# Gate and up products of a feed-forward layer by Strassen's scheme, on one core

## The chip, the cores and the metric

The kernel runs on one core of a Trainium2 chip. The core has a matrix engine (PE, with its loads of weights as PEld), a vector engine (DVE), a scalar engine (ACT), GpSimd (POOL) and a queue of transfers that SyncE (SP) issues. The metric is the device time of one execution in microseconds, less is better.

## What is computed

A trunk of two layers on 512 tokens of width 1024. Each layer has a feed-forward layer (FFN), a mixer and a second FFN, each on the RMS-normalised x and added to x.

```python
def rmsnorm(x, g):
    y = xf * lax.rsqrt(jnp.mean(xf * xf, axis=-1, keepdims=True) + EPS)
    return (y * g.astype(jnp.float32)).astype(x.dtype)
def swiglu_ffn(x, w_gu, w_down):
    gate, up = jnp.split(x @ w_gu, 2, axis=-1)
    return (jax.nn.silu(gate) * up) @ w_down
```

D_FF is 2816. The first mixer (stage ab) is a recurrence beside a chunked mLSTM, the second (stage nsa) is attention with a compressed, a selected and a window branch.

## The kernel before

The stages run in the order f0a, ab, f0b, f1a, nsa, f1b; four of them are FFNs. x lies transposed in eight tiles X of 128 channels x 512 tokens. Every product keeps fp32 accuracy by splitting both operands into a high part (a copy rounded to the matmul's type, on ACT) and a low part (the difference, on DVE), and by three matmuls, high x high, high x low and low x high: `mm3`, L169 to L171 of the profile.

An FFN goes through 22 tiles j of 128 hidden channels. For each j two weight tiles of 128 x 1024 (gate and up) are brought in by `wload`: one transfer of 512 KB, the high part on ACT (L164), the low part on DVE (L165). Then 16 `mm3`, that is 48 matmuls of 128 x 512, make the gate and the up rows. x stands in these products without its norm; 1/rms of each token (the row R, 128 x 512, the same on each partition) is multiplied to the results in `hidden` (L235, L237), where Silu, the product and the split into high and low follow. The sum for R (`rms_sum`, L133) and its spread along the free axis (`rms_row`, L145) stand on PE between the products of j=1, so that the next stage's products need not wait for the norm. The down product then takes all 22 hidden tiles, for each of the eight tiles of X 66 matmuls, and the result is added to X (L274). For the next stage `prep` (L99, L100) splits the new X and `square` (L109, L111) adds its squares, on ACT and POOL.

A scheduler with priorities puts the instructions of each engine in order; where the code says `manual_schedule(engines=PE_ONLY)`, PE's order is the written one. `high_priority(offset=...)` in the loads makes weights come ahead. Within an engine, order is fixed when the program is built, and each instruction waits for what it needs.

In nsa the scores of 128 queries are computed by `scores`: for each of two heads a selected and compressed part (`slc`) and a window part (`win`), each as a product of 128 rows (high parts, L755, L762) and one of 64 rows (low parts, L756, L763) into one PSUM tile, 64 of each kind. Between them stand turns of other products.

## Time and profile before

| | |
|---|---|
| median of 3 runs | 2132.83 us (2132.11 to 2137.12) |
| profiled execution, from first to last instruction | 2130.4 us |
| PE busy | 2097.7 us, 98% |
| PEld, DVE, ACT, POOL busy | 78%, 48%, 38%, 13% |
| mean granted clock of PE | 0.990 |
| DMA, mean over the span | 85 GB/s |

A busy share is the time in which an engine had an instruction under way. The chain is followed back from the last instruction, each step to what released it. The groups by line sum instructions of the same kind, with their mean length and the idle time ahead of them. Times in the timeline and in the windows count from the first instruction.

### The profile page before, as it was taken

How to read it: one execution, taken by the hardware profiler on the slowest of the kernel's cores; microseconds unless marked ns; L12 is line 12 of the kernel's file. 1: busy time of each engine (PE TensorE's matmuls, PEld its weight loads, DVE VectorE, ACT ScalarE, POOL GpSimd, SP SyncE). 2: the span in 40 equal slices, each digit the busy share in tenths (PEclk: the TensorE clock that was granted, in tenths of full speed). 3: DMA queues.
4: the chain of work that ended last, by engine and by line, in shares of the span. 5: the costliest groups of instructions: out<-in, count | busy, mean ns of one | idle time of the engine just before them, and what ended most of it. 6: DMA issues, size and time to landing. Idle time of an engine off the chain costs nothing.

```text
span 2130.4 us, 23902 instructions
## 1 busy us (share of the span) xinstructions
PE 2097.7 (98%) x9304; PEld 1672.3 (78%) x9304; DVE 1016.8 (48%) x1685; ACT 803.0 (38%) x1368; POOL 271.8 (13%) x290
## 2 busy tenths in 40 slices
PE   8999999989999999999999999999999999999997
PEld 7888888767888888888888888877766678888886
DVE  5444423587644444333444432324767664444332
ACT  4322322454532323223322322235777753323221
POOL 3000000242020000000000000003555430000001
PEclk9999999999999999999999999999999999999998
DMA  4232233222132232332232233331000023222331
GB/s 149 90 99 95 91 91 100 89 77 82 54 99 94 95 99 90 91 100 97 89 99 97 89 100 91 129 109 37 23 11 21 16 75 102 95 99 89 96 95 67
DMA packets 53970, 181.66 MB, mean 85 GB/s; under 512 B 6113, under 2 KB 6881, under 8 KB 53857
## 3 DMA queue, kind: packets, MB, share of 16 engines
q1 hardware_dynamic: 53712, 180.05, 26.6%
q8 instruction: 73, 1.20, 0.2%
q14 instruction: 41, 0.33, 0.0%
...
## 4 chain that ended last, share of the span: by engine, by line
PE 95%; DVE 2%; issue 1%; ACT 1%; POOL 1%; DMA 0%; SPq 0%; POOLq 0%; ACTq 0%; DVEq 0%
PE ps L169 20%; PE ps L171 19%; PE ps L170 19%; PE pt L171 8%; PE pt L169 8%; PE pt L170 8%; PE px L801 2%; PE pt L817 2%; PE pt L594 2%; PE ps L756 1%; PE ps L763 1%; PE pt L818 1%; PE ps L220 1%; PE ps L221 1%; PE ps L222 1%
## 5 line engine op out<-in xcount | busy, mean ns | idle before, releaser
L164 ACT ACTIVATE whi<-raw 128x1024 fp32r<-128x1024 f32 (+2 forms) x340 | 345.8, 1019 | 1062.8 <-PE ps L170 654.0
L165 DVE TENSOR_TENSOR wlo<-raw,whi 128x1024 fp32r<-128x1024 f32 (+2 forms) x310 | 368.3, 1189 | 349.9 <-ACT whi L164 344.7
L169 PE MATMUL ps<-x,whi 128*128 128x512 f32 x1008 | 407.0, 404 | 1.9 <-ACT x L99 1.9
L171 PE MATMUL ps<-x,wlo 128*128 128x512 f32 x1008 | 399.3, 396 | 0.0
L170 PE MATMUL ps<-x,whi 128*128 128x512 f32 x1008 | 395.9, 393 | 0.4 <-DVE x L100 0.3
L171 PE MATMUL pt<-x,wlo 128*128 128x512 f32 x704 | 278.3, 395 | 2.0 <-POOL wlo L951 2.0
L170 PE MATMUL ps<-h,whi 128*128 128x512 f32 x704 | 277.4, 394 | 0.0
L169 PE MATMUL ps<-h,whi 128*128 128x512 f32 x704 | 277.2, 394 | 0.0
L169 PE MATMUL pt<-x,whi 128*128 128x512 f32 x704 | 276.8, 393 | 0.0
L171 PE MATMUL ps<-h,wlo 128*128 128x512 f32 x704 | 276.4, 393 | 0.0
L170 PE MATMUL pt<-x,whi 128*128 128x512 f32 x704 | 275.6, 392 | 0.0
L111 POOL TENSOR_TENSOR acc<-acc,t 128x512 f32<-128x512 f32 x48 | 71.4, 1487 | 1461.4 <-ACT t L109 1447.0
L169 PEld LDWEIGHTS ps<-x,whi 128*128 128x128 f32 x1008 | 189.8, 188 | 46.5 <-issue 2.8
L170 PEld LDWEIGHTS ps<-x,whi 128*128 128x128 f32 x1008 | 190.1, 189 | 44.1 <-DVE x L100 1.9
L171 PEld LDWEIGHTS ps<-x,wlo 128*128 128x128 f32 x1008 | 189.8, 188 | 44.2 <-issue 0.2
L237 DVE TENSOR_TENSOR t<-pt,R 128x512 f32<-128x512 f32 x88 | 60.8, 691 | 279.5 <-PE pt L171 279.4
L171 PEld LDWEIGHTS pt<-x,wlo 128*128 128x128 f32 x704 | 132.3, 188 | 32.8 <-POOL wlo L951 2.5
L170 PEld LDWEIGHTS pt<-x,whi 128*128 128x128 f32 x704 | 132.4, 188 | 31.5
L171 PEld LDWEIGHTS ps<-h,wlo 128*128 128x128 f32 x704 | 132.3, 188 | 31.0
L169 PEld LDWEIGHTS ps<-h,whi 128*128 128x128 f32 x704 | 132.1, 188 | 31.3
L170 PEld LDWEIGHTS ps<-h,whi 128*128 128x128 f32 x704 | 132.1, 188 | 30.4
L169 PEld LDWEIGHTS pt<-x,whi 128*128 128x128 f32 x704 | 132.3, 188 | 29.6
...
## 6 DMA issues: line engine op xcount, KB each, us to landing
...
raw<-nsa_out SPq DMA_DIRECT2D x16, 256.0 KB, 2.7
X<-xT SPq DMA_DIRECT2D x8, 256.0 KB, 5.3
```

The lines of the kernel that those rows point to most:

```text
L111: nc.gpsimd.tensor_add(acc, acc, sq)
L164: nc.scalar.activation(hi[:, :n], raw[:, :n], AF.Copy)
L165: (eng or nc.vector).tensor_sub(lo[:, :n], raw[:, :n], hi[:, :n].bitcast(F32))
L169: nc.tensor.matmul(ps, wh, xh, start=start, stop=False)
L170: nc.tensor.matmul(ps, wh, xl, start=False, stop=False)
L171: nc.tensor.matmul(ps, wl, xh, start=False, stop=stop)
L220: nc.tensor.matmul(pss[t], xh, wh, start=k == 0, stop=False)
L221: nc.tensor.matmul(pss[t], xl, wh, start=False, stop=False)
L237: nc.vector.tensor_mul(t2, pu, R)
L594: nc.tensor.matmul(p2[m][:, :155].rearrange("p (g n) -> p g n", g=5), w[:, q * 256 + m * P:q * 256 + (m + 1) * P], tt[:, :, n:n + 8 * 30 + ...
L801: nc.tensor.transpose(px[:kk, (2 * m + r) * P:(2 * m + r + 1) * P], pt[r][b][:, off:off + kk], ident)
L817: nc.tensor.matmul(po[0][:, :2 * P], v, ph[:kk, ms], start=n == 0 and m == 0, stop=False)
```

## The change

The gate and up products of the pairs j = 2 to 21 become Strassen's scheme (Winograd's form): gate and up weights of a j are one matrix of 2 x 2 quarters (k halves x gate or up), x is one of 2 x 2 quarters (k halves x token halves), and 7 products of quarters take the place of 8. j = 0 and 1 stay as before. After them x is normalised with R on DVE, and seven operands are made of its quarters, B11, Q7, Q6, B21, Q4, Q5, B22 (`quarters`), each in a high and a low part. On the side of the weights `sload` brings in 1 MB for each j in three transfers into a pair of r buffers (ra, rc; two such pairs in turn), makes four combinations on POOL (L289 to L292), and splits all in four steps, three of 128 x 1024 and one of 128 x 512, on ACT (L303) and DVE (L304), into five slots used in turn. A product is 12 matmuls of 128 x 256. Partial results are read from PSUM by ACT (L387, L389, L393) and added by DVE (L395, L384, L380); the last product of a pair, B22, is put between Q7 and Q6 of the next pair. The down product goes in three parts, after j = 7, 15 and 21, each added to X. The norm's sum goes two products earlier (13 for 15) except in f0a. In nsa, `both` issues the two high products first and the two low ones after, in two PSUM tiles. Comments that the change strips are left out here.

```diff
-        def ffn(wgu, wd, x, hb, nxt, first=None):
+        QS = ("B11", "Q7", "Q6", "B21", "Q4", "Q5", "B22")
+        WS = {"B11": (0, 0), "Q7": (0, 1), "Q6": (1, 0), "B21": (1, 1), "Q4": (2, 0), "Q5": (2, 1), "B22": (3, 0)}
+        H = T // 2
+        def quarters(qb, tmp):
+            Q = {}
+            xn = [blk(b, F32, f"xn{b}")[:, :4 * T].rearrange("p (k t) -> p k t", k=4) for b in tmp[:2]]
+            sm = blk(tmp[2], F32, "qs")[:, :4 * T].rearrange("p (s k t) -> p s k t", s=2, k=4)
+            B = {f"B{h + 1}{t + 1}": xn[h][:, :, t * H:(t + 1) * H] for h in range(2) for t in range(2)}
+            gname = plan[current[0]]
+            def norm(h):
+                for k in range(4):
+                    nc.vector.scalar_tensor_tensor(xn[h][:, k], X[4 * h + k], col(gname, 4 * h + k), R,
+                                                   op0=OP.mult, op1=OP.mult)
+            def split(name, src, neg):
+                t = blk(qb[QS.index(name)], F32R, f"q{name}")
+                hi, lo = (t[:, n * 4 * H:(n + 1) * 4 * H].rearrange("p (k t) -> p k t", k=4) for n in range(2))
+                nc.scalar.activation(hi, src, AF.Copy, scale=-1.0 if neg else 1.0)
+                if neg:
+                    nc.vector.scalar_tensor_tensor(lo, src, -1.0, hi.bitcast(F32), op0=OP.mult, op1=OP.subtract)
+                else:
+                    nc.vector.tensor_sub(lo, src, hi.bitcast(F32))
+                Q[name] = hi, lo
+            def sums(n):
+                if n == 0:
+                    nc.vector.tensor_sub(sm[:, 0], B["B12"], B["B22"])
+                    split("Q7", sm[:, 0], False)
+                if n == 1:
+                    nc.gpsimd.tensor_sub(sm[:, 1], B["B12"], B["B11"])
+                    nc.vector.tensor_sub(sm[:, 0], B["B22"], sm[:, 1])
+                    split("Q6", sm[:, 0], False)
+                if n == 2:
+                    split("Q5", sm[:, 1], False)
+                    nc.gpsimd.tensor_sub(sm[:, 1], B["B21"], sm[:, 0])
+                    split("Q4", sm[:, 1], False)
+            return Q, [lambda: norm(0), lambda: split("B11", B["B11"], True), lambda: norm(1), lambda: sums(0),
+                       lambda: sums(1), lambda: split("B21", B["B21"], True), lambda: sums(2),
+                       lambda: split("B22", B["B22"], True)]
+        def sload(w, rb, wx):
+            with tc.high_priority(offset=SAHEAD):
+                n = turns[0]
...
+                nc.sync.dma_start(ra[:, 0:4:3], w[0].rearrange("p (s c) -> p s c", s=2))
+                nc.sync.dma_start(rc[:, 3], w[1][:, :T])
+                nc.sync.dma_start(rc[:, 0], w[1][:, T:])
+                nc.gpsimd.tensor_add(ra[:, 1], ra[:, 0], rc[:, 3])
+                nc.gpsimd.tensor_add(rc[:, 1], rc[:, 0], rc[:, 3])
+                nc.gpsimd.tensor_add(ra[:, 2], ra[:, 0], rc[:, 1])
+                nc.gpsimd.tensor_add(rc[:, 2], ra[:, 3], ra[:, 2])
+                out = []
+                for src, m in ((ra[:, 0:2], 2), (ra[:, 2:4], 2), (rc[:, 0:2], 2), (rc[:, 2:3], 1)):
+                    at = turns[0] % 5
...
+                    nc.scalar.activation(hi[:, :m * T], src, AF.Copy)
+                    nc.vector.tensor_sub(lo[:, :m * T], src, hi[:, :m * T].bitcast(F32))
...
-            at = 19 if first else 15
+            at = 19 if first else 13
...
-            for j in range(JT):
+            for j in range(2):
...
+            Q, steps = quarters(qb, hb[1:4])
+            for n, f in enumerate(steps):
+                f()
+                if n in (4, 6):
+                    hidden(*wait.pop(0))
+            def product(ps, W, name, start):
+                wh, wl = W[name]
+                xh, xl = Q[name]
+                for k in range(4):
+                    ks = slice(k * P, (k + 1) * P)
+                    mm3(ps[:, :H], wh[:, ks], wl[:, ks], xh[:, k], xl[:, k], start and k == 0, k == 3, not start)
+            def pair(j, left, more):
+                W = sload(wgu[j], rb, wx)
+                a, b, e = psum(), psum(), psum2()
...
+                def last():
+                    product(a, W, "B22", False)
+                    nc.scalar.activation(t1[:, hi], a[:, :H], AF.Silu, scale=-1.0)
+                    nc.vector.tensor_mul(t2, t1, t2)
+                    down(j, t2)
+                def turn():
+                    product(a, W, "Q5", False)
+                    nc.vector.tensor_add(t2[:, hi], a[:, :H], t2[:, hi])
+                def other():
+                    product(e, W, "Q4", False)
+                    nc.vector.tensor_add(t2[:, lo], e[:, :H], t2[:, lo])
+                product(a, W, "B11", True)
+                nc.scalar.activation(t1[:, lo], a[:, :H], AF.Copy)
+                product(e, W, "Q7", True)
+                nc.scalar.activation(t2[:, hi], e[:, :H], AF.Copy)
+                if left:
+                    left()
+                product(a, W, "Q6", False)
+                nc.scalar.activation(t2[:, lo], a[:, :H], AF.Copy)
+                product(b, W, "B21", True)
+                nc.vector.tensor_add(t1[:, lo], b[:, :H], t1[:, lo])
+                nc.scalar.activation(t1[:, lo], t1[:, lo], AF.Silu, scale=-1.0)
+                if more:
+                    other()
+                    turn()
+                    return last
+                turn()
+                other()
+                last()
+            for j0 in range(0, JT, NH):
+                j1 = min(JT, j0 + NH)
+                with tc.manual_schedule(engines=PE_ONLY):
+                    left = None
+                    for j in range(max(2, j0), j1):
+                        left = pair(j, left, j < j1 - 1)
...
+                for i in range(KT):
+                    ps = psum()
+                    hi, lo = wload(wd[i, :, j0 * P:j1 * P], (j1 - j0) * P)
...
+                    nc.vector.scalar_tensor_tensor(X[i], ps, 0.5, X[i], op0=OP.mult, op1=OP.add)
+                    if j1 == JT:
+                        nxt(i)
...
-                def slc(r):
...
-                def win(r):
...
+                def both(r):
                     q = QH[g][2 * r + par]
...
+                    p1, p2 = psum(), psum()
+                    nc.tensor.matmul(p1[:, :n1], q[:, qs], KH[g][:, :n1], start=True, stop=False)
+                    nc.tensor.matmul(p2[:, :n2], q[:, qs], KWH[g][:, w0:w0 + n2], start=True, stop=False)
+                    nc.tensor.matmul(p1[:, :n1], q[rr, qs], KL[g // 2][rr, :n1], start=False, stop=True)
+                    nc.tensor.matmul(p2[:, :n2], q[rr, qs], KWL[g // 2][rr, w0:w0 + n2], start=False, stop=True)
...
-                return [lambda: slc(0), lambda: win(0), lambda: slc(1), last]
...
+                return [lambda: both(0), last]
```

In f0a the transfers for pair 2 stand first on SP, ahead of X and the first weights. In the code after the change, lines have moved: `mm3` is L171 to L173, the low part of `wload` is L166, `hidden` is L327 to L330 with `down` at L321 and L322.

DVE in f0b, from behind the row sum on. Before, in order (t1 and t2 are the hidden rows, R the row of 1/rms, wlo the low part of weights, h the low part of hidden rows):

```order
L235 TENSOR_TENSOR t1_4261<-ps_4123,R_84 128x512
L237 TENSOR_TENSOR t2_4262<-pt_4124,R_84 128x512
L235 TENSOR_TENSOR t1_4269<-ps_4202,R_84 128x512
L238 TENSOR_TENSOR t2_4262<-t1_4261,t2_4262 128x512
L165 TENSOR_TENSOR wlo_4286<-raw_4283,whi_4285 128x1024
L241 TENSOR_TENSOR h4_4100<-t2_4262,h4_4100 128x512
L237 TENSOR_TENSOR t2_4270<-pt_4203,R_84 128x512
L238 TENSOR_TENSOR t2_4270<-t1_4269,t2_4270 128x512
L165 TENSOR_TENSOR wlo_4350<-raw_4347,whi_4349 128x1024
L241 TENSOR_TENSOR h4_4100<-t2_4270,h4_4100 128x512
```

After, at the same place, from the fourth of the eight normalisations on (xn8, xn9 are the halves of normalised x, X its tiles, r0 and r1 the r buffers, q... the operands by their names, qs the differences); the three normalisations ahead of it are like it:

```order
L248 SCALAR_TENSOR_TENSOR xn8_5392<-X3_73,prm_78,R_84 128x512
L248 SCALAR_TENSOR_TENSOR xn9_5393<-X4_74,prm_78,R_84 128x512
L248 SCALAR_TENSOR_TENSOR xn9_5393<-X5_75,prm_78,R_84 128x512
L304 TENSOR_TENSOR wlo_5460<-r0_5446,whi_5459 128x1024
L256 SCALAR_TENSOR_TENSOR qB11_5399<-xn8_5392,qB11_5399 128x1024
L248 SCALAR_TENSOR_TENSOR xn9_5393<-X6_76,prm_78,R_84 128x512
L248 SCALAR_TENSOR_TENSOR xn9_5393<-X7_77,prm_78,R_84 128x512
L327 TENSOR_TENSOR t1_5415<-ps_5254,R_84 128x512
L263 TENSOR_TENSOR qs_5394<-xn8_5392,xn9_5393 128x1024
L329 TENSOR_TENSOR t2_5416<-pt_5255,R_84 128x512
L304 TENSOR_TENSOR wlo_5464<-r1_5447,whi_5463 128x1024
L258 TENSOR_TENSOR qQ7_5407<-qs_5394,qQ7_5407 128x1024
```

and directly behind these:

```order
L256 SCALAR_TENSOR_TENSOR qB21_5423<-xn9_5393,qB21_5423 128x1024
L267 TENSOR_TENSOR qs_5394<-xn9_5393,qs_5394 128x1024
L330 TENSOR_TENSOR t2_5416<-t1_5415,t2_5416 128x512
L304 TENSOR_TENSOR wlo_5567<-r0_5554,whi_5566 128x1024
L258 TENSOR_TENSOR qQ6_5412<-qs_5394,qQ6_5412 128x1024
L322 TENSOR_TENSOR h7_5238<-t2_5416,h7_5238 128x512
L258 TENSOR_TENSOR qQ5_5426<-qs_5394,qQ5_5426 128x1024
L327 TENSOR_TENSOR t1_5433<-ps_5333,R_84 128x512
L329 TENSOR_TENSOR t2_5434<-pt_5334,R_84 128x512
L256 SCALAR_TENSOR_TENSOR qB22_5441<-xn9_5393,qB22_5441 128x1024
L330 TENSOR_TENSOR t2_5434<-t1_5433,t2_5434 128x512
L258 TENSOR_TENSOR qQ4_5430<-qs_5394,qQ4_5430 128x1024
```

The hidden rows of j = 0 and 1 now stand among the normalisations and the operands' low parts, and three weight splits stand there too.

POOL in f0b behind the last of the next norm's sums. Before, nothing follows there until the next stage's norm. After:

```order
L266 TENSOR_TENSOR qs_5394<-xn8_5392 128x1024
L289 TENSOR_TENSOR r0_5678<-r0_5678,r1_5679 128x512
L290 TENSOR_TENSOR r1_5679<-r1_5679 128x512
L291 TENSOR_TENSOR r0_5678<-r0_5678,r1_5679 128x512
L292 TENSOR_TENSOR r1_5679<-r0_5678 128x512
L271 TENSOR_TENSOR qs_5394<-xn9_5393,qs_5394 128x1024
L289 TENSOR_TENSOR r0_5801<-r0_5801,r1_5802 128x512
```

Two of the operands' differences (L266, L271) and the combinations of the weights of pairs 4 and 5 stand in one row on POOL.

DVE in f0b in two later pairs (t1, t2 the hidden rows, ps and pt PSUM tiles, wx3, wx4 and wlo weight slots). Before:

```order
L235 TENSOR_TENSOR t1_4339<-ps_4289,R_84 128x512
L165 TENSOR_TENSOR wlo_4356<-raw_4353,whi_4355 128x1024
L237 TENSOR_TENSOR t2_4340<-pt_4290,R_84 128x512
L238 TENSOR_TENSOR t2_4340<-t1_4339,t2_4340 128x512
L165 TENSOR_TENSOR wlo_4420<-raw_4417,whi_4419 128x1024
L241 TENSOR_TENSOR h5_4101<-t2_4340,h5_4101 128x512
```

After:

```order
L375 TENSOR_TENSOR t2_5582<-t1_5581,t2_5582 128x512
L395 TENSOR_TENSOR t1_5704<-ps_5702,t1_5704 128x256
L322 TENSOR_TENSOR h8_5239<-t2_5582,h8_5239 128x512
L384 TENSOR_TENSOR t2_5705<-pt_5703,t2_5705 128x256
L304 TENSOR_TENSOR wx4_5817<-r1_5802,wx4_5817 128x1024
L380 TENSOR_TENSOR t2_5705<-ps_5701,t2_5705 128x256
L304 TENSOR_TENSOR wlo_5821<-r1_5802,whi_5820 128x512
L304 TENSOR_TENSOR wlo_5934<-r0_5924,whi_5933 128x1024
L304 TENSOR_TENSOR wlo_5938<-r0_5924,whi_5937 128x1024
L375 TENSOR_TENSOR t2_5705<-t1_5704,t2_5705 128x512
L395 TENSOR_TENSOR t1_5827<-ps_5825,t1_5827 128x256
L322 TENSOR_TENSOR h9_5240<-t2_5705,h9_5240 128x512
```

A j has four weight splits L304 in place of two L165, and three additions of 256 columns (L395, L384, L380) in place of the two products with R; L380 stands between splits.

PE in nsa (ps are scores, kh and k the keys' high and low parts, q the queries, the rest is other work). Before:

```order
L755 MATMUL ps_10201<-kh4_8716,q11_9475 128x256
L756 MATMUL ps_10201<-k5_8717,q11_9475 128x256
L169 MATMUL ps_10023<-x1_8073,whi_10019 128x512
L170 MATMUL ps_10023<-x3_8075,whi_10019 128x512
L171 MATMUL ps_10023<-x1_8073,wlo_10020 128x512
L817 MATMUL pt_10173<-t1_10183,v8_8720 128x256
L818 MATMUL pt_10173<-t2_10184,v8_8720 128x256
L817 MATMUL pt_10173<-t1_10183,v9_8721 128x256
L818 MATMUL pt_10173<-t2_10184,v9_8721 128x256
L801 MATMUL px_10213<-ident_80,pb16_8724 32x128 x2
L762 MATMUL ps_10220<-k6_8718,q11_9475 128x256
L763 MATMUL ps_10220<-k7_8719,q11_9475 128x256
```

After:

```order
L903 MATMUL ps_13586<-kh4_12130,q11_12944 128x256
L904 MATMUL ps_13587<-k6_12132,q11_12944 128x256
L905 MATMUL ps_13586<-k5_12131,q11_12944 128x256
L906 MATMUL ps_13587<-k7_12133,q11_12944 128x256
L961 MATMUL pt_13572<-t1_13563,v9_12135 128x256
L962 MATMUL pt_13572<-t2_13564,v9_12135 128x256
L961 MATMUL pt_13572<-t1_13563,v9_12135 128x256
L962 MATMUL pt_13572<-t2_13564,v9_12135 128x256
```

The two products of high parts (L903, L904) now follow each other, and so do the two of low parts on 64 rows (L905, L906).

## Rows read from the trace of the kernel before

**Rows 1.** The page: busy time of the engines, and the chain that ended last.

```profile
PE 2097.7 (98%) x9304; PEld 1672.3 (78%) x9304; DVE 1016.8 (48%) x1685; ACT 803.0 (38%) x1368; POOL 271.8 (13%) x290
...
PE 95%; DVE 2%; issue 1%; ACT 1%; POOL 1%; DMA 0%; SPq 0%; POOLq 0%; ACTq 0%; DVEq 0%
```

**Rows 2.** Window of f0b: length, busy PE, PEld, DVE, ACT, POOL, clock, DMA.

```profile
613.00:982.00 369.00, 369.00 (x1606) 299.98 (x1605) 149.21 (x177) 109.03 (x133) 9.74 (x7) 1.00 0.30 94
```

**Rows 3.** Timeline of PE in f0b: start, length, engine, line.

```profile
700.45 0.40 PE L169 MATMUL pt<-x,whi 128*128 128x512 f32 x1
...
700.92 0.39 PE L171 MATMUL pt<-x,wlo 128*128 128x512 f32 x1
```

**Rows 4.** Timeline in nsa: products of 256 columns, loads of weights.

```profile
1650.58 0.28 PE L817 MATMUL pt<-t,v 128*128 128x256 f32 x1
1650.58 0.19 PEld L818 LDWEIGHTS pt<-t,v 128*128 128x128 f32 x1
...
1650.93 0.28 PE L818 MATMUL pt<-t,v 128*128 128x256 f32 x1
```

**Rows 5.** Timeline of DVE in f0b: two weight splits in turn.

```profile
625.88 2.36 DVE L165 TENSOR_TENSOR wlo<-raw,whi 128x1024 fp32r<-128x1024 f32 x2 [8.83 <-ACT whi L164]
```

**Rows 6.** Groups of DVE's instructions: busy, mean ns, idle before.

```profile
L274 DVE SCALAR_TENSOR_TENSOR X<-ps,X 128x512 f32<-128x512 f32 x32 | 22.2, 692 | 75.4 <-PE ps L171 75.4
...
L806 DVE TENSOR_TENSOR t<-px,t 128x256 fp32r<-128x256 f32 x8 | 3.4, 421 | 0.3
```

**Rows 7.** Timeline of ab: DVE and POOL.

```profile
420.79 1.87 POOL L413 TENSOR_TENSOR qT<-qT,t 128x512 f32<-128x512 f32 x1 [2.13 <-ACT t L412]
...
421.50 1.70 DVE L391 SCALAR_TENSOR_TENSOR misc<-misc 4x512 f32<-4x512 f32 x1
...
422.60 1.76 POOL L358 TENSOR_TENSOR rg<-rg,rg 128x512 f32<-128x512 f32 x1
...
423.24 1.67 DVE L340 SCALAR_TENSOR_TENSOR kT<-t,prm,kT 128x510 f32<-128x510 f32 x1
```

**Rows 8.** Groups of POOL's instructions.

```profile
L165 POOL TENSOR_TENSOR wlo<-raw,whi 128x1024 fp32r<-128x1024 f32 x22 | 53.9, 2451 | 159.2 <-ACT whi L164 149.6 <-PE pt L145 9.5
```

**Rows 9.** Timeline of the end of nsa: POOL and DVE.

```profile
1740.01 3.56 POOL L111 TENSOR_TENSOR acc<-acc,t 128x512 f32<-128x512 f32 x2 [1.80 <-ACT t L109]
...
1742.33 0.68 DVE L850 TENSOR_TENSOR X<-ps,X 128x512 f32<-128x512 f32 x1
```

**Rows 10.** Timeline of PE in ab, with the idle time ahead.

```profile
436.86 3.75 PE L354 MATMUL pt<-rg,num 128*128 128x512 f32 x4 [7.28 <-DVE rg L340]
```

**Rows 11.** Windows in ab: the column ahead of DMA is the clock.

```profile
434.00:436.00 2.00, 0.00 (x0) 0.00 (x0) 1.97 (x5) 1.99 (x3) 0.00 (x0) 0.63 0.00 0
436.00:438.00 2.00, 1.15 (x2) 0.66 (x3) 2.00 (x3) 2.00 (x3) 0.00 (x0) 0.50 0.00 0
...
442.00:444.00 2.00, 2.00 (x10) 1.65 (x9) 0.64 (x2) 1.85 (x3) 0.00 (x0) 1.00 0.65 231
```

**Rows 12.** Groups of ACT's instructions.

```profile
L164 ACT ACTIVATE whi<-raw 128x1024 fp32r<-128x1024 f32 x292 | 308.8, 1059 | 957.2 <-PE ps L170 565.2 <-issue 355.1 <-PE pt L170 12.5
L240 ACT ACTIVATE h<-t 128x512 fp32r<-128x512 f32 x88 | 55.8, 634 | 59.7 <-DVE t L238 59.7
```

**Rows 13.** The page: DMA issues, median us from issue to landing.

```profile
raw<-nsa_out SPq DMA_DIRECT2D x16, 256.0 KB, 2.7
```

**Rows 14.** Window of the scores in nsa.

```profile
1480.00:1720.00 240.00, 234.81 (x1204) 168.60 (x1203) 170.55 (x605) 178.73 (x537) 123.07 (x177) 0.99 0.06 20
```

**Rows 15.** Timeline of PE in nsa: products of 128 and 64 rows.

```profile
1500.03 0.34 PE L755 MATMUL ps<-kh,q 128*128 128x384 f32 x1
1500.30 0.44 PE L756 MATMUL ps<-k,q 64*128 64x384 f32 x1
1500.67 0.39 PE L817 MATMUL pt<-t,v 128*128 128x256 f32 x1
1500.90 0.28 PE L818 MATMUL pt<-t,v 128*128 128x256 f32 x1
```

More of the change, by code (lines that the diff above doesn't have):

```diff
@@ new lines, in build @@
+        turns = [0]
+        def sload(w, rb, wx):
+            with tc.high_priority(offset=SAHEAD):
+                n = turns[0]
+                ra, rc = (blk(rb[2 * (n // 4 % 2) + i], F32, f"r{i}")[:, :4 * T].rearrange("p (s c) -> p s c", s=4)
+                          for i in range(2))
+                nc.sync.dma_start(ra[:, 0:4:3], w[0].rearrange("p (s c) -> p s c", s=2))
[8 more added lines that the diff above has]
+                    at = turns[0] % 5
+                    turns[0] += 1
+                    if at < 3:
+                        hi, lo = wp.tile([P, CW], F32R, name="whi"), wp.tile([P, CW], F32R, name="wlo")
+                    else:
+                        t = blk(wx[at - 3], F32R, f"wx{at}")
+                        hi, lo = t[:, :CW], t[:, CW:2 * CW]
+                    src = src.rearrange("p s c -> p (s c)")
+                    nc.scalar.activation(hi[:, :m * T], src, AF.Copy)
+                    nc.vector.tensor_sub(lo[:, :m * T], src, hi[:, :m * T].bitcast(F32))
+                    out += [(hi[:, k * T:(k + 1) * T], lo[:, k * T:(k + 1) * T]) for k in range(m)]
+            return dict(zip(("B11", "Q7", "Q6", "B21", "Q4", "Q5", "B22"), out))
@@ L226, in ffn, with down @@
+        current = [None]
+        def ffn(wgu, wd, x, lay, nxt, first=None):
+            qb, hb, rb, wx = lay
             hs = slots(hb, F32R, "h")
             HH, HL = hs[0::2], hs[1::2]
-            at = 19 if first else 15
+            NH = len(HH)
+            at = 19 if first else 13
             wait = []
+            def down(j, t2):
+                hh, hl = HH[j % NH], HL[j % NH]
+                nc.scalar.activation(hh, t2, AF.Copy)
+                nc.vector.tensor_sub(hl, t2, hh.bitcast(F32))
@@ L258, in ffn @@
                 wait.append((j, pg, pu))
-                if 16 * j + 15 < at + 5:
-                    continue
-                for args in wait:
-                    hidden(*args)
-                wait.clear()
-            roots(HH[JT - 1].bitcast(F32))
-            for i in range(KT):
-                ps = psum()
-                for c0 in range(0, JT, 8):
-                    n = min(8, JT - c0)
-                    hi, lo = wload(wd[i, :, c0 * P:(c0 + n) * P], n * P)
-                    for k in range(n):
-                        kk = c0 + k
-                        mm3(ps, hi[:, k * P:(k + 1) * P], lo[:, k * P:(k + 1) * P], HH[kk], HL[kk],
-                            kk == 0, kk == JT - 1)
-                nc.vector.scalar_tensor_tensor(X[i], ps, 0.5, X[i], op0=OP.mult, op1=OP.add)
-                nxt(i)
+            Q, steps = quarters(qb, hb[1:4])
@@ new lines, in ffn @@
+            for j0 in range(0, JT, NH):
+                j1 = min(JT, j0 + NH)
+                with tc.manual_schedule(engines=PE_ONLY):
+                    left = None
+                    for j in range(max(2, j0), j1):
+                        left = pair(j, left, j < j1 - 1)
+                if j1 == JT:
+                    roots(HH[(JT - 1) % NH].bitcast(F32))
+                for i in range(KT):
+                    ps = psum()
+                    hi, lo = wload(wd[i, :, j0 * P:j1 * P], (j1 - j0) * P)
+                    for k in range(j1 - j0):
+                        mm3(ps, hi[:, k * P:(k + 1) * P], lo[:, k * P:(k + 1) * P], HH[k], HL[k],
+                            k == 0, k == j1 - j0 - 1)
+                    nc.vector.scalar_tensor_tensor(X[i], ps, 0.5, X[i], op0=OP.mult, op1=OP.add)
+                    if j1 == JT:
+                        nxt(i)
@@ L982, in build @@
                 f = {"f0a": 0, "f0b": 1, "f1a": 2, "f1b": 3}[st]
-                hb = list(range(4, 15)) if base == 0 else list(range(4)) + list(range(8, 15))
-                ffn(a["wgu"][f], a["wd"][f], x, hb, nxt, first if n == 0 else None)
+                lay = (((4, 5, 6, 0, 1, 2, 3), (7, 8, 9, 10), (13, 14, 15, 16), (11, 12)) if base == 0 else
+                       ((14, 15, 16, 4, 5, 6, 7), (2, 3, 0, 1), (8, 9, 10, 11), (12, 13)))
+                current[0] = st
+                ffn(a["wgu"][f], a["wd"][f], x, lay, nxt, first if n == 0 else None)
             base = nbase
```

33 lines of the change are left out of this document (14 added, 19 removed).

## The prediction

> **What bounds the kernel now.** I read the page first: PE is busy 98% of the span, and the chain that ended last is 95% PE [rows 1]. The reader is to see that no other engine comes near: DVE 48%, ACT 38%, POOL 13%. Then the FFN's stretch: in f0b the 369 us have PE busy for 369 us, DVE for 149, POOL for 10 [rows 2]. So in the FFNs the kernel is as long as its matmuls are, and a matmul that goes away is time gained, as long as DVE, ACT and POOL keep up with what takes its place. The question of this case is whether they do, so the later groups are durations on these three and how two of them disturb each other.
>
> **The matmuls.** A 128x512 matmul starts 0.231 us after the one before (700.45 to 700.92 in two steps) [rows 3]; a 128x256 one, each with its own 128x128 weights, 0.117 us (1650.58 to 1650.93 in three steps), and its weight load of 0.19 us is hidden [rows 4]. Before, one j has 48 of the first: 11.09 us. A pair has 7 products x 4 x 3 = 84 of the second: 9.83 us. Gain 1.26 us for each of 20 pairs in 4 FFNs, 80 in all: **-101 us**; as the rows show bursts of four and not of 84, I take **-98** (bounds -95 and -102).
>
> **The start of each FFN.** The first pair can't go on before the combinations of x exist, and these begin only when R is there. R comes from the row reduction in j=1, after which 13 of j=1's 16 steps of three matmuls are left (7 in f0a): 13 x 3 x 0.231 = 9.0 us (4.9). B11, Q7, Q6 and B21 of pair 2 are 4 x 1.40 = 5.6 us more, so PE has 14.6 us of work until it needs Q4 (10.5 in f0a). DVE's order after R, up to the low part of Q4, holds 8 normalisations L248, 7 low parts L256 and L258 and 2 differences of 128x1024, 3 weight splits L304, and 7 steps of the hidden rows of j=0 and 1 (the rows of DVE in the change's section). Prices: 1024 wide 1.18 us (2.36 for two that stand back to back) [rows 5], 512 wide 0.69, 256 wide 0.42 [rows 6]. 15 x 0.69 + 12 x 1.18 = 24.5 us.
> To this POOL adds time. Where DVE reads two operands from SBUF and POOL works too, the trace shows that they take turns: from 420.79 to 424.91 POOL, DVE, POOL, DVE end in turn (422.66, 423.20, 424.36, 424.91): POOL 1.16 us behind DVE's end, DVE 0.54 and 0.55 behind POOL's, so that instructions that would take 0.7 show 1.70 and 1.67 [rows 7]. A DVE instruction with an operand in PSUM is not held: L850 takes its usual 0.68 in the middle of two POOL adds that last from 1740.01 to 1743.57 [rows 9]. L266 and L271 hold twice 2.3 us (1024 wide, 2.45 on POOL [rows 8], less what the 512-wide ones lose in turn), of which 1.4 pass beside L327 and L329, which read PSUM: 3.2 us. The four additions for pair 4 hold 4.6 us if they fall into this stretch; their transfers end about when Q7 does. So Q4 is ready 27.7 to 32.3 us after R, and PE stands for 13.1 to 17.7 us. I take 15, and 19 in f0a: 3 x 15 + 19 = **+64** (56 to 75). Before, nothing waits there.
> Such a pause also lowers the clock: PE was idle for 7.28 us up to 436.86 [rows 10], and the granted clock fell from 1.00 of 2.4 GHz to its lower level, 1.2 GHz: 0.63 in the window from 434 to 436, 0.50 in the next one, 1.00 again from 442 to 444 [rows 11]. PE worked there for some 5 us at half speed. The stall here comes in three pieces of 4 to 7 us. 2 us for each FFN: **+8** (0 if these pieces leave the clock alone, 20 if more than one of each three pays it).
>
> **The steady pairs.** PE's cycle is 9.83 us. ACT has 3 of 1.06 and, with the 256-wide ones put at a 512-wide one's 0.63, 7 of that: under 7.6 us [rows 12], and no bound. DVE has 3 x 1.18 + 3 x 0.69 + 3 x 0.42 = 6.9 us, and POOL four additions that hold 4 x 1.16 = 4.6. These exclude each other except beside the three 256-wide sums with an operand in PSUM: 10.2 us if those are all covered, 11.5 if none is, half a us less if each 512-wide one behind POOL takes 0.55. That is about PE's cycle or above. So I follow the loop that closes from one L380 to the next. L380(j) releases B22(j): 1.40 on PE; this frees weights' slots: hi 1.06, lo 1.18, at 3.64. Then L375 0.69, the hidden row's high part L321 on ACT 0.63, the next split's hi 1.06 and lo 1.18, L322 0.69, L384 and L380 0.84: 8.7 us, 1.1 less than PE's cycle. The additions come into it: L304's last part behind L380 (0.69) frees the r buffer, whose 256 KB take 2.7 us from issue to landing [rows 13], so that POOL is ready at 3.4 us or later, just when L375 is. If L375 goes first, two additions pass until the split, one ahead of L322: 3.64 + 0.69 + 2.32 + 1.18 + 1.16 + 0.55 + 0.84 = 10.4, 0.5 us over PE's cycle. If POOL goes first, 1.16 for its first addition comes on top and L375 takes 0.55: 11.4, 1.6 over. If the transfer lasts longer or POOL's hop does, only one or two fall into the loop, and it stays under 9.83. The additions run in about 13 of the 20 cycles of an FFN (4, 6 and 3 in its parts: a part's first pair and a half is split during the down product before it, and its last ones have no further pair to add for). I take the middle one, since additions that come late push their own trigger later: 13 x 4 x 0.5 = **+26** (0 to 83).
>
> **The rest.** The down product has the same 528 matmuls; its 16 more updates of X, 0.69 each on DVE [rows 6], stand beside turns of 24, 24 and 18 matmuls; in the shortest, 18 x 0.231 = 4.2 us, DVE has an update, x's low part and a weight split, under 2 x 0.69 + 1.18 = 2.6, and POOL holds 1.16: nothing (0 to 6). At the start of f0a 1 MB for pair 2 stands on SP ahead of X and the first weights. The best rate in a window of the trace is 231 GB/s [rows 11]: 4.5 us, a little hidden: **+4** (0 to 6). Scores: where a product of 64 rows follows one of 128, and 128 again after it, starts lie 0.27, 0.37 and 0.23 apart, against 0.174 for 384 columns (an estimate between the two sizes of rows 3 and 4) and 0.117 for 256 [rows 15]: 0.10 + 0.20 + 0.11 = 0.41 us for each change to 64 rows and back. 128 such before, 64 after: up to 26 us. PE is busy there for 235 of 240 us [rows 14], so most of it counts; but two scores at a time ask more of DVE (171 us of 240) and PSUM: **-18** (0 to -26).
>
> **Sum.** -98 + 64 + 8 + 26 + 4 - 18 = -14. Against the profiled 2130.4 us that is 2116; the median of the runs is 2.4 above the span: **2119 us**, 0.7% less. What a measurement of this kernel can tell from no change is about 0.3%, 6 us.
>
> **The rivals.**
> *POOL first (slower).* The loop closes at 11.4 us in the cycles with additions: 52 x 1.6 = 83 for 26, +43 in all, 2176 us. For it: POOL's transfer and L375 come within 0.3 us of each other, and from 420.79 on the one that waited always went next [rows 7]. Against: a later transfer moves it out. It decides from 0.77 us a cycle on (26 + 14 over 52). The Trainium skill, SBUF — State Buffer, "Who interferes with whom", states the same: of a DVE and a POOL instruction at their shared port the first to issue holds it for its whole length and the other is blocked. Rows 7 agree with it; it speaks against putting this change's additions on POOL.
> *Short starts (much faster).* Additions for pair 4 stay out of the start, the pieces don't touch the clock, and the loop stays under PE's cycle: -98 + 56 + 0 + 5 + 2 - 22 = -57, 2076 us. Against: DVE's 24.5 us alone are 10 more than PE's work.
> *Even.* Gain and pauses cancel within 6 us: any 14 us more than I took, such as 0.3 us a cycle.
> *The change doesn't give its gain:* if each 128x256 matmul waited for its 0.19 us load in long runs, a pair would be 84 x 0.19 = 16 us, 4.9 more than before: 80 x 4.9 and the +84 of the sum's other terms, some 475 us longer. Nothing in rows 4 shows it.
>
> **Chances.** Forecast (2085 to 2126) 0.36, POOL first (2140 to 2200) 0.37 with starts longer than I took counted in, short starts 0.11, even 0.12, no gain 0.04. The forecast is the middle of my sum and with short starts makes faster 0.47; same 0.12; slower 0.41. As both signs hold much, the range goes from the short starts to a loop at 1.6 us with the rest as summed, with some of its tail: 2070 to 2195; the forecast's own is 2085 to 2126.
>
> **What would show it.** Right: 128x256 starts 0.117 apart inside a product; PE idle three times in the first pair of each FFN, ended by DVE's L258 and L256, 15 us together; POOL's L289 to L292 at 1.2 us and more, and L304 longer than 1.23; PE's wait for L380 in the pairs, 0.5 us each; windows of the scores shorter by 15 to 20 us. Wrong: a wait for L380 over 0.8 us in most pairs (POOL first); no PE idle over 3 us at the FFNs' starts (short starts); steps of 0.19 us (no gain).

## The result: slower by 1.0%, and the profile after

The changed kernel takes 2158.98 us (median of 4 runs, 2156.03 to 2160.55), the kernel before on the same chip 2134.39 us (2132.11 to 2137.12): ratio 1.0104, 95% interval 1.0081 to 1.0128. The profiled execution has 2156.0 us and a mean granted clock of 0.965; before it was 0.990.

The page, engines and chain, as in [rows 1]:

```profile
PE 2034.5 (94%) x12184; PEld 1772.0 (82%) x12184; DVE 1467.9 (68%) x2057; ACT 1040.1 (48%) x1876; POOL 876.8 (41%) x618
...
PE 71%; DVE 15%; issue 6%; ACT 5%; POOL 2%; DMA 1%; SPq 0%; POOLq 0%; ACTq 0%; DVEq 0%
```

PE's busy time fell by 63 us and its idle time rose by 89. The chain, 95% PE before, is 71% PE; DVE holds 15% of it, ACT 5%.

Windows by stage (length; busy PE, PEld, DVE, ACT, POOL; clock; DMA): up to the first pair, f0a's pairs of the first, second and third part, ab with f0b's plain j, the first parts of f0b, f1a, f1b, and nsa with f1b's plain j:

```profile
0.00:45.70 45.70, 35.06 (x133) 26.73 (x133) 30.99 (x32) 20.53 (x33) 32.48 (x31) 0.85 0.53 174
45.70:129.80 84.10, 65.94 (x505) 64.13 (x504) 75.33 (x72) 44.83 (x69) 46.76 (x26) 0.86 0.24 77
174.40:256.60 82.20, 80.61 (x674) 79.77 (x673) 70.15 (x69) 46.11 (x78) 55.50 (x32) 1.00 0.33 110
301.30:367.50 66.20, 62.06 (x506) 61.26 (x505) 51.59 (x78) 36.42 (x60) 27.61 (x15) 0.97 0.21 62
400.70:668.70 268.00, 257.65 (x1118) 205.70 (x1116) 181.31 (x215) 124.77 (x183) 80.50 (x44) 0.93 0.24 78
668.70:751.10 82.40, 68.62 (x505) 66.31 (x504) 72.05 (x71) 43.61 (x68) 46.47 (x25) 0.88 0.26 85
1043.20:1124.50 81.30, 67.30 (x506) 65.08 (x505) 70.47 (x71) 43.66 (x68) 47.04 (x25) 0.90 0.27 86
1793.10:1873.60 80.50, 67.15 (x506) 64.78 (x505) 68.74 (x71) 43.67 (x68) 45.04 (x24) 0.87 0.27 88
1390.60:1793.10 402.50, 390.70 (x1970) 301.65 (x1968) 258.02 (x753) 246.58 (x655) 164.15 (x210) 1.00 0.16 53
```

The same stretches of before, for the first, for ab and for nsa:

```profile
0.00:36.60 36.60, 30.77 (x132) 24.36 (x133) 18.12 (x29) 21.60 (x34) 17.29 (x22) 0.95 0.55 175
380.70:638.10 257.40, 249.55 (x1118) 199.17 (x1117) 177.11 (x236) 126.80 (x187) 67.17 (x38) 0.97 0.24 79
1350.20:1767.70 417.50, 412.01 (x1970) 306.69 (x1969) 249.27 (x749) 249.04 (x655) 149.55 (x202) 0.99 0.16 52
```

Six pairs are 504 products, 59.0 us at 0.117 us. A first part takes 80.5 to 84.1, with PE idle for 13 to 18 us and a clock of 0.86 to 0.90. A second part (672 products, 78.6 us) takes 82, at a clock of 1.00. ab, in which nothing was changed, is 10.6 us longer in these two traces; nsa is 15.0 us shorter, and the time ahead of the first pair 9.1 longer.

PE's waits: total, times, longest:

```profile
PE ps L171 <- DVE t L380: 22.7, 37, 1.8
PE pt L171 <- ACT qQ L254: 20.4, 7, 4.6
PE ps L171 <- ACT t L387: 13.5, 4, 5.3
PE pt L172 <- DVE qQ L258: 10.9, 7, 3.8
```

PE in the first pair of f0b (start, length, and in brackets the idle time ahead and who ended it):

```profile
670.19 0.28 PE L172 MATMUL ps<-qB,whi 128*128 128x256 f32 x1
670.30 0.28 PE L173 MATMUL ps<-qB,wlo 128*128 128x256 f32 x1
673.42 0.43 PE L171 MATMUL pt<-qQ,whi 128*128 128x256 f32 x1 [2.84 <-ACT qQ L254]
674.98 0.58 PE L172 MATMUL pt<-qQ,whi 128*128 128x256 f32 x1 [1.13 <-DVE qQ L258]
...
676.21 0.41 PE L171 MATMUL pt<-qQ,whi 128*128 128x256 f32 x1
676.43 0.41 PE L172 MATMUL pt<-qQ,whi 128*128 128x256 f32 x1
...
680.42 0.58 PE L171 MATMUL ps<-qQ,whi 128*128 128x256 f32 x1 [2.73 <-ACT t L387]
682.26 0.58 PE L172 MATMUL ps<-qQ,whi 128*128 128x256 f32 x1 [1.26 <-DVE qQ L258]
...
689.69 0.38 PE L171 MATMUL pt<-qQ,whi 128*128 128x256 f32 x1 [2.21 <-ACT qQ L254]
691.42 0.58 PE L172 MATMUL pt<-qQ,whi 128*128 128x256 f32 x1 [1.35 <-DVE qQ L258]
```

The reader is to see three pauses, ahead of Q7, Q6 and Q4, each in two pieces: the first ended by an operand's high part (L254) or by a copy on ACT (L387), the second by its low part (L258). Between the first products of 670 the steps are 0.11 us; between those of 676 they are 0.21 to 0.22. Windows of the same stretch (the column ahead of DMA is the granted clock):

```profile
674.00:682.00 8.00, 3.30 (x12) 2.71 (x12) 7.13 (x6) 5.31 (x8) 5.43 (x3) 0.50 0.24 80
688.00:690.00 2.00, 0.31 (x1) 0.19 (x1) 2.00 (x2) 1.06 (x1) 0.55 (x1) 1.00 0.02 4
692.00:696.00 4.00, 4.00 (x21) 4.00 (x20) 1.86 (x3) 0.53 (x2) 0.00 (x0) 0.50 0.01 4
```

So the clock is at its lower level, 1.2 GHz, from the pause ahead of Q7 on. It is up again when PE has run the rest of Q6 and B21 without a pause, and falls once more with the pause ahead of Q4.

### The profile page after: what moved, and what is told of

It is laid out like the page before. It is cut to its first block, busy times and chain, and to the rows that moved or that the text cites. A ratio compares the mean times of both kernels' runs of the same rounds, so it can differ in the third digit from the quotient of the medians.

```text
span 2156.0 us, 31290 instructions
## 1 busy us (share of the span) xinstructions
PE 2034.5 (94%) x12184; PEld 1772.0 (82%) x12184; DVE 1467.9 (68%) x2057; ACT 1040.1 (48%) x1876; POOL 876.8 (41%) x618
## 4 chain that ended last, share of the span: by engine, by line
PE 71%; DVE 15%; issue 6%; ACT 5%; POOL 2%; DMA 1%; SPq 0%; POOLq 0%; ACTq 0%; DVEq 0%
PE ps L171 18%; PE ps L172 17%; PE ps L173 17%; PE pt L172 3%; DVE wlo L304 2%; PE pt L173 2%; PE pt L171 2%; PE px L945 2%; DVE t L375 2%; PE pt L740 2%; DVE xn L248 1%; ACT wx L303 1%; DVE wlo L166 1%; PE pt L961 1%; DVE qQ L258 1%
## 5 line engine op out<-in xcount | busy, mean ns | idle before, releaser
L289 POOL TENSOR_TENSOR r<-r,r 128x512 f32<-128x512 f32 x80 | 137.9, 1724 | 651.6 <-DMA r<-wgu 588.3
L165 ACT ACTIVATE whi<-raw 128x1024 fp32r<-128x1024 f32 (+2 forms) x180 | 176.7, 982 | 363.9 <-PE ps L172 249.3
L303 ACT ACTIVATE whi<-r 128x1024 fp32r<-128x1024 f32 x192 | 182.7, 952 | 236.1 <-PE ps L172 172.3
L304 DVE TENSOR_TENSOR wlo<-r,whi 128x1024 fp32r<-128x1024 f32 x192 | 254.6, 1328 | 54.4 <-ACT whi L303 52.6
L171 PE MATMUL ps<-h,whi 128*128 128x512 f32 x704 | 277.1, 394 | 0.0
L173 PE MATMUL ps<-h,wlo 128*128 128x512 f32 x704 | 276.6, 393 | 0.0
L166 DVE TENSOR_TENSOR wlo<-raw,whi 128x1024 fp32r<-128x1024 f32 (+2 forms) x150 | 184.7, 1232 | 79.3 <-ACT whi L165 74.5
L304 DVE TENSOR_TENSOR wx<-r,wx 128x1024 fp32r<-128x1024 f32 (+1 forms) x128 | 185.7, 1451 | 51.2 <-ACT wx L303 49.6
L171 PE MATMUL ps<-qB,whi 128*128 128x256 f32 x576 | 166.4, 289 | 10.5 <-DVE t L380 10.5
L172 PE MATMUL ps<-qB,whi 128*128 128x256 f32 x576 | 163.8, 284 | 2.4 <-DVE qB L256 2.1
L173 PE MATMUL ps<-qB,wlo 128*128 128x256 f32 x576 | 163.3, 284 | 0.0
L303 ACT ACTIVATE wx<-r 128x1024 fp32r<-128x1024 f32 (+1 forms) x128 | 121.4, 948 | 80.8 <-PE pt L173 36.3
L171 PE MATMUL ps<-x,whi 128*128 128x512 f32 x368 | 154.6, 420 | 3.2 <-ACT whi L1094 3.2
L173 PEld LDWEIGHTS ps<-h,wlo 128*128 128x128 f32 x704 | 132.4, 188 | 30.7
L171 PEld LDWEIGHTS ps<-h,whi 128*128 128x128 f32 x704 | 132.2, 188 | 30.7
L290 POOL TENSOR_TENSOR r<-r 128x512 f32<-128x512 f32 x80 | 146.1, 1826 | 17.2 <-DMA r<-wgu 17.1
L291 POOL TENSOR_TENSOR r<-r,r 128x512 f32<-128x512 f32 x80 | 150.6, 1883 | 5.8
L292 POOL TENSOR_TENSOR r<-r 128x512 f32<-128x512 f32 x80 | 147.0, 1837 | 6.1
```

Of the source, the lines that this page charges most:

```text
L165: nc.scalar.activation(hi[:, :n], raw[:, :n], AF.Copy)
L166: (eng or nc.vector).tensor_sub(lo[:, :n], raw[:, :n], hi[:, :n].bitcast(F32))
L171: nc.tensor.matmul(ps, wh, xh, start=start, stop=False, skip_group_check=on)
L172: nc.tensor.matmul(ps, wh, xl, start=False, stop=False, skip_group_check=on)
L173: nc.tensor.matmul(ps, wl, xh, start=False, stop=stop, skip_group_check=on)
L289: nc.gpsimd.tensor_add(ra[:, 1], ra[:, 0], rc[:, 3])
```

## The experiments

Each is timed against the kernel before on the same chip (2134.6, 2135.8 and 2136.3 us in the three groups).

**Paired scores alone** (`scores`): the kernel before with `both` in place of `slc` and `win`.

```diff
-                return [lambda: slc(0), lambda: win(0), lambda: slc(1), last]
+                return [lambda: both(0), last]
```

> The kernel before with the paired scores alone. If a change of rows from 128 to 64 and back costs what it shows in the rows (0.41 us, 64 fewer): up to 26 us less, 16 to 18 as nsa shows in the changed kernel, 2117 us for 2134. Rival: nsa is shorter in the changed kernel only because its clock or its neighbours differ there: 2134.

2116.95 us, ratio 0.9918 (0.9893 to 0.9942): 17.6 us less. The gain is of the pairing and not of the neighbours.

**No additions** (`noadds`):

```diff
-                nc.gpsimd.tensor_add(ra[:, 1], ra[:, 0], rc[:, 3])
...
-                for src, m in ((ra[:, 0:2], 2), (ra[:, 2:4], 2), (rc[:, 0:2], 2), (rc[:, 2:3], 1)):
+                for src, m in ((ra[:, 0:4:3], 2), (ra[:, 0:4:3], 2), (rc[:, 0:4:3], 2), (rc[:, 0:1], 1)):
```

> The changed kernel without the four additions of weights on POOL; the splits read loaded quarters in their place, so the gate and up rows are of other weights. Theory S: the pairs behind the first part lose their 20 to 30 us over 0.117 us a product, the starts keep 10 us of pauses and more in each FFN, since DVE's own list is 24.5 us: 2115 to 2130 us. Theory L: starts and pairs both come down to PE's own time, pauses under 5 us in each start: below 2090 us.

2091.56 us (0.9796, 0.9765 to 0.9828): 67 us less than the changed kernel. Its windows up to the first pair, of ab, of f0b's first and second part:

```profile
0.00:37.50 37.50, 31.12 (x133) 24.12 (x133) 26.75 (x32) 20.68 (x33) 17.90 (x23) 0.95 0.64 212
377.90:634.80 256.90, 249.07 (x1118) 198.86 (x1116) 177.82 (x215) 124.83 (x183) 69.02 (x35) 0.97 0.25 81
634.80:708.40 73.60, 65.62 (x506) 63.67 (x505) 55.03 (x71) 43.64 (x68) 2.39 (x1) 0.91 0.29 96
752.90:832.50 79.60, 79.60 (x674) 79.57 (x673) 52.23 (x71) 46.38 (x78) 0.00 (x0) 1.00 0.34 113
```

By spans: the four first parts give back 28 us together, the later parts 22, the time ahead of the first pair 8, ab 11. The second part is within 1 us of its products' time, with PE busy throughout; f0b's first part is still 14.6 us longer than its products. So each theory holds a part: the pairs come down and the starts keep their pauses, as S said, but the total is near L's, since the time came back in four places and not in one (whether ab's 11 belong to the additions is taken up below).

**Three plain j** (`plain3`):

```diff
-            for j in range(2):
+            for j in range(3):
...
-                if n in (4, 6):
+                if n in (2, 4, 6):
...
-                    for j in range(max(2, j0), j1):
+                    for j in range(max(3, j0), j1):
```

> The changed kernel with three plain j ahead of the pairs instead of two, the rows of j = 0, 1, 2 made among the operands. Theory S: PE has 11.1 us more work while the operands are made, so the pauses fall by 10 to 11 us in each FFN and with them most of the time at the lower clock (4 us); one pair less costs 1.3 us: 4 x (11 + 4 - 1.3) = 55 us less, 2104 us. Theory L: DVE has more to do in the start, POOL's additions as many; the pairs after it lose what the start gains; 2150 to 2165.

2135.33 us (1.0008, 0.9991 to 1.0025): 24 us less than the changed kernel, where S said 55. In f0b the pause for Q7 is gone, that for Q6 is 2.6 us, but one of 5.2 stays ahead of Q4, ended by a copy on ACT (L389). A window in it:

```profile
682.00:685.00 3.00, 0.00 (x0) 0.00 (x0) 0.13 (x1) 0.02 (x1) 2.94 (x2) 0.82 0.54 173
```

DVE and ACT do nothing, POOL is busy throughout. On ACT that copy stands behind Q4's high part, which waits for Q4's difference (L271), and on POOL this stands behind the additions for the next pairs. This led to the next three.

**The differences on DVE** (`dvesum`; with three and four plain j, `plain3d` and `plain4d`):

```diff
-                    nc.gpsimd.tensor_sub(sm[:, 1], B["B12"], B["B11"])
+                    nc.vector.tensor_sub(sm[:, 1], B["B12"], B["B11"])
...
-                    nc.gpsimd.tensor_sub(sm[:, 1], B["B21"], sm[:, 0])
+                    nc.vector.tensor_sub(sm[:, 1], B["B21"], sm[:, 0])
```

> The changed kernel with the two differences that POOL makes of x's quarters (for Q6, Q5 and for Q4) on DVE, 1.2 us each there for 2.4 on POOL. Theory R (POOL's row makes Q4 late: its difference stands behind four additions of weights): the pause ahead of Q4 (4.3 us) falls by 2 to 4 us in each FFN, 2143 to 2151. Theory D (DVE's own list sets the start): 2.4 us more on DVE, pauses 2 us longer, 2160 to 2170.

2144.61 us (1.0034, 1.0017 to 1.0050), 14 us less: theory R's number. The pause ahead of Q4 in f0b fell from 4.3 to 1.8 us, as R said. But the one at Q6 rose from 5.0 to 7.8, as D said of DVE's longer list, so that f0b's pauses fell by only 1 us in sum; over the four FFNs some 10 us of pauses and 7 of lower clock went.

> Three plain j, and the two differences on DVE. With three plain j one pause of 5.5 us was left ahead of Q4, while DVE and ACT stood idle and POOL worked. Theory R: it falls below 2 us, and the clock stays up: 2135 less 4 x 5 to 6, 2110 to 2117. Theory D: DVE's list is as long, the pause moves to Q7 or Q6: 2130 to 2140.

2122.75 us (0.9925, 0.9905 to 0.9945): 13 us less than with three plain j alone, in the direction of R but short of its number.

> Four plain j, and the two differences on DVE. If the start's pauses are all that PE lacks against DVE's list, none over 1 us is left with 22 us more of PE's work ahead; the fourth plain j costs 1.3 us in each FFN. 2100 to 2112. If additions and splits of later pairs fill DVE in any case, it gains nothing against three: 2112 to 2125.

2106.49 us (0.9856, 0.9831 to 0.9880), as said: the fastest here that computes the reference, 29 us below the kernel before and 10 below the paired scores alone. In the first pair of an FFN I take each start-to-start step of PE from the trace, less 0.117 us; what is left of steps from 0.20 to 0.27 us goes to the lower clock, what is left of longer ones is pause. In us:

| plain j, differences on | pauses f0a, f0b, f1a, f1b | sum | lower clock, sum |
|---|---|---|---|
| 2, POOL (changed kernel) | 17.6, 14.3, 14.2, 15.0 | 61 | 18 |
| 2, POOL, no additions | 14.7, 10.8, 10.8, 10.6 | 47 | 14 |
| 2, DVE | 12.5, 13.2, 13.2, 12.6 | 52 | 11 |
| 3, POOL | 13.1, 9.2, 8.0, 8.0 | 38 | 12 |
| 3, DVE | 9.2, 7.5, 5.1, 5.7 | 28 | 8 |
| 4, DVE | 1.7, 4.4, 0, 2.8 | 9 | 3 |

A plain j more takes 19 to 24 us of pauses away in the four FFNs, half of the 44 that its 11.1 us would allow. Its own weight splits and hidden rows come onto DVE's list as well, which is a likely reason that no run separates; ahead of the fourth j, only 28 us were left to take.

**The pauses filled** (`fill`, `fill2`, `fill3`), products without use into a PSUM tile of their own:

```diff
+                fill(32)
                 product(e, W, "Q7", True)
...
+                fill(32)
                 product(a, W, "Q6", False)
...
+                    fill(26)
                     other()
```

> The changed kernel with PE kept busy in the pauses of each FFN's first pair: 32, 32 and 26 products of 128x256 without use ahead of Q7, Q6 and Q4. Theory S (the pauses for the operands of x, and the lower clock that follows them, are the loss): the pauses of 12 to 16 us stay, filled, but the clock stays at its upper level; 4 to 6 us less in each FFN, some 2140 us for 2159. Theory L (the turns of DVE and POOL at their port are the loss, the clock only goes along with idle time): nothing is gained, 2159, or up to 10 us more where a filling outlasts its pause.

2175.40 us (1.0192, 1.0162 to 1.0222).

> As the run with the pauses filled, but the filling products take both operands from B11 of x, so that they hold no slot of weights (the first form held the slot that the next pair's split waits for, 9 us). Theory C (the lower clock in the first pair costs 4 to 6 us in each FFN besides the pauses): the granted clock stays at its upper level in the first parts, and these are 76 to 80 us long for 80 to 84: 2137 to 2147 us. Theory P (only the pauses cost; PE would wait at either clock): first parts as long as before, 2155 to 2165.

2180.02 us (1.0195, 1.0180 to 1.0211). In both, other work shifted on DVE and ACT as well, and a pause of 9 to 10 us came ahead of Q6. In it, in the second form, DVE and ACT are idle and POOL works, as the window shows; the line behind it is the first of POOL's additions, just before:

```profile
683.00:688.00 5.00, 0.00 (x0) 0.00 (x0) 0.00 (x0) 0.00 (x0) 4.84 (x5) 0.63 0.34 104
```

```profile
676.96 6.38 POOL L289 TENSOR_TENSOR r<-r,r 128x512 f32<-128x512 f32 x1 [10.37 <-DMA r<-wgu]
```

That addition lasted 6.38 us and ended about 1 us after DVE's row of steps with two operands in SBUF, which ran to 682.2; three more additions followed, and only then Q4's difference (L271), behind which the copy that releases Q6 stood on ACT. So both say nothing of the clock, but once more that POOL's row makes x's operands late. The third form fills the one pause whose filling leaves the other engines' orders as they are.

> The changed kernel with 24 products of 128x256 without use in the pause ahead of Q4 alone (4.3 us in f0b, f1a and f1b); the order of DVE, ACT, POOL and SP is that of the changed kernel. Theory C (after the pause Q4, Q5 and the next products run at the lower clock): the clock stays up behind the filling, Q4 starts as before, and some 20 to 30 products of 0.21 become 0.117: 2 to 3 us less in each of the three FFNs, 6 to 9 in all, 2150 to 2153. Theory P (the clock costs nothing besides): 2159 or a little more.

2160.94 us (1.0112, 1.0093 to 1.0132): no change against the changed kernel. Windows of f1a behind Q4, filled and not filled:

```profile
1064.00:1070.00 6.00, 5.80 (x49) 5.80 (x50) 3.66 (x7) 2.32 (x4) 0.00 (x0) 1.00 0.06 12
```

```profile
1066.00:1072.00 6.00, 6.00 (x37) 6.00 (x38) 3.55 (x6) 1.74 (x3) 0.00 (x0) 0.72 0.01 3
```

The clock does stay up, 49 products in 6 us for 37, and by the steps the lower clock costs 11 us in the four first pairs for 18: theory C's 6. But the first parts of f0b, f1a and f1b are only 2.1, 1.2 and 0.5 us shorter, f0a's is 1.4 longer and nsa with f1b's plain j 3.3, so the time as a whole is theory P's. The lower clock's cost in the starts is thus a count of slow steps; that as much comes back when the clock stays up, no run shows.

**B22 behind Q6** (`late22`; with four plain j `plain4dl`; that with a lower priority for the loads of f0a's first pairs, `plain4dls`):

```diff
-                if left:
-                    left()
                 product(a, W, "Q6", False)
                 nc.scalar.activation(t2[:, lo], a[:, :H], AF.Copy)
+                if left:
+                    left()
```

> The changed kernel with B22 of the pair before moved behind Q6 of the next pair instead of ahead of it. It needs L380 1.4 us later. Theory W (PE's waits for L380, 37 of 0.6 us on average and 22.7 together, are the loss of the steady pairs): they fall below 5 us, 18 us less, 2141. Theory G (DVE and POOL together are slower than PE, so the wait only moves to the splits, which now get their slots 1.4 us later): 2155 to 2165, with waits for L304 or L303.

2265.01 us (1.0595, 1.0571 to 1.0620), 106 us more than the changed kernel. PE's waits:

```profile
PE ps L171 <- ACT t L387: 102.7, 57, 5.3
...
PE ps L171 <- DVE t L380: 18.4, 12, 3.5
```

Neither theory had this: Q6 writes on into the PSUM tile of B11, which ACT must have copied (L387), and that copy stands behind other work on ACT. The last of that work, L396, itself waits for DVE (L395), which comes behind weight splits there:

```profile
ACT t L396 <- DVE t L395: 123.6, 61, 3.1
```

B22 ahead of Q6 gave the copy 1.4 us more. The waits for L380 became fewer, 12 for 37.

> Four plain j, the differences on DVE, and B22 behind Q6. Theory W: the waits for L380 (19.5 us with four plain j) fall below 5: 2106 less 14 to 16, 2091. Theory G: 2103 to 2110.

2190.09 us (1.0244, 1.0220 to 1.0267): the same wait for L387, 82 us.

> The same with the transfers for f0a's first two pairs behind x and the first weights on SP instead of ahead of them. The first pair of f0a then begins 4 to 8 us earlier, as f0a's first products did without additions (8 us) and in the kernel before (9 us): 2082 to 2089 if B22 behind Q6 gains, 2098 to 2104 if not. If only the additions and not the transfers held f0a's start: as without, 0.

2190.84 us (1.0255, 1.0232 to 1.0279), no change. But the edit moved nothing: with four plain j the first transfer of f0a's first pair already stood behind x and the first weights. Its issue in `plain4dl`, in `plain4dls`, and in the run without additions:

```profile
18.08 0.63 SPq L286 DMA_DIRECT2D r<-wgu  x1
```

```profile
17.55 0.65 SPq L286 DMA_DIRECT2D r<-wgu  x1
```

```profile
0.81 0.65 SPq L286 DMA_DIRECT2D r<-wgu  x1
```

All engines' instructions stand in the same order in the first two, so this run tests nothing of the transfers; it is a second execution of the same program. The run without additions answers the question: there the transfers come first, as in the changed kernel, and the first pair begins at 37.5 us, for 36.6 us to the same place before and 45.7 in the changed kernel.

## Why the prediction was wrong

The sum ended at -14 us, the profiled spans differ by +25.6. The forecast sign came from gains of 116 us (matmuls and scores) less costs of 102, and no single term turns it. Its steps one by one:

- **The matmuls** (-98): right. The later parts without additions have steps of 0.117 to 0.118 us, by which 80 pairs save 94 to 101.
- **The start, pauses** (+64): right in size, its cause only in part, so the close agreement is partly luck. 61 us in the first pairs, 17.6 in f0a and 14.2 to 15.0 in the others, for 19 and 15 (the table above). The working had DVE's list, with POOL's holds in it, as the only bound; the waits show ACT's and POOL's rows in it too: Q6 waited first for a copy that ACT had behind other work (L387), and with the differences on DVE instead of POOL 10 us of the pauses went, though DVE's list grew.
- **The clock in the start** (+8): the step that failed by most. The sum took 2 us for each FFN. By the steps it is 18 us, 3.6 to 5.5 in each FFN: 37 to 57 products between and behind the pauses run at 0.21 us. In f0b the clock fell with the first pause, stayed down through the second and fell again with the third (the windows above). The mechanism was right and the size was not; 18 lies inside the bounds that the prediction gave the term, and without these 10 us the kernel would still have been some 15 slower.
- **Left out of the sum: ab** (0 without a reason, measured +10.6). The same products there run at the lower clock for longer: the two windows below lie inside the one long stretch of before and of after.

```profile
524.00:533.00 9.00, 9.00 (x30) 6.98 (x31) 3.41 (x7) 2.45 (x9) 0.00 (x0) 0.50 0.00 0
```

```profile
541.00:562.00 21.00, 21.00 (x72) 16.30 (x72) 5.79 (x12) 7.36 (x25) 0.25 (x1) 0.50 0.07 25
```

Added up over ab in steps of 2 us, 17.1 us are at 1.2 GHz before and 37.5 after; half of the difference is 10.2 us, about all that ab lost. In the run without additions it is 17.1 again, and ab 256.9 us. That the change causes this is not shown. Each kernel has one trace, and the two executions of one program, `plain4dl` and `plain4dls`, differ in the same stretch; these are 20 us of each, from 142 us behind the start of ab on:

```profile
546.00:566.00 20.00, 20.00 (x74) 16.37 (x72) 6.71 (x13) 7.13 (x24) 0.00 (x0) 0.50 0.05 22
```

```profile
549.00:569.00 20.00, 20.00 (x108) 16.65 (x109) 9.05 (x20) 8.74 (x31) 0.00 (x0) 0.75 0.04 18
```

In one 27.3 us of ab are at 1.2 GHz, in the other 17.1, and ab is 4.5 us longer in the first. The kernel before, too, took 2129.97 to 2142.15 us in its runs, with mean clocks from 0.991 down to 0.984, and its trace is one of the shorter ones. On the other hand the changed kernel, the three with filled pauses and the one with the differences on DVE all have 37.5. What decides the length of the stretch stays open.
- **f0a's first products** (+4, measured +9.1): the term has the wrong cause. Without additions 8 us came back while the transfers still stood ahead of x, so the additions for f0a's first pairs, between POOL's weights and squares and beside DVE's splits of x, are the cause. About half of it is the clock again: PE was busy for 35.06 us there, for 30.77 before, at a granted clock of 0.85 for 0.95.
- **The steady pairs** (+26, 0 to 83): right, 6 us short. All steps over 0.27 us behind the first pairs come to 32 us, 23 of them waits for L380, 37 times and never over 1.8; without the additions 3 are left. The rival of POOL going first did not come, as a wait is 0.6 us and not 1.6 a cycle; that the kernel ended on that rival's side has another reason.
- **Scores** (-18): 17.6 alone, 15.0 in the changed kernel.
- **The down product** (0): right; 44.5 to 44.8 us for 192 products, PE's own time (192 steps of 0.231 are 44.4).

Of the 40 us between sum and measurement, 20 are the lower clock (10 in the starts, 10 in ab), 5 f0a's first products, 6 the steady pairs, 3 the scores; the rest is in steps a little over 0.117 us, less what the matmuls and the pauses came out better than in the sum. The turns of DVE and POOL cost both sides: additions that took 1.26 us with DVE idle (f0a's first) last 1.7 to 1.9, and the 512-wide L375 and L322 1.2 to 1.3 instead of 0.69; without the additions the same two take 0.69 us. The Trainium skill (SBUF — State Buffer, "Who interferes with whom") states such turns at a port that the two share; these rows agree. The rows of POOL and of DVE:

```profile
L291 POOL TENSOR_TENSOR r<-r,r 128x512 f32<-128x512 f32 x80 | 150.6, 1883 | 5.8
...
L289 POOL TENSOR_TENSOR r<-r,r 128x512 f32<-128x512 f32 x80 | 137.9, 1724 | 651.6 <-DMA r<-wgu 588.3 <-DVE wlo L304 28.4 <-issue 20.4
```

```profile
L304 DVE TENSOR_TENSOR wlo<-r,whi 128x1024 fp32r<-128x1024 f32 x144 | 206.1, 1431 | 53.4 <-ACT whi L303 51.7
...
L322 DVE TENSOR_TENSOR h<-t,h 128x512 fp32r<-128x512 f32 x88 | 106.7, 1213 | 16.1 <-ACT h L321 16.1
L375 DVE TENSOR_TENSOR t<-t,t 128x512 f32<-128x512 f32 x80 | 104.1, 1301 | 7.3 <-ACT t L374 7.2
```

Without the additions the kernel is 67 us faster: 29 in the steady pairs, 14 in the pauses and 3 to 4 in the clock of the starts, 8 ahead of the first pair, 11 in ab (which may be the execution's), 2 in nsa.
